# New estimates, a hold-back margin and four column groups in the planner of a hybrid attention and mLSTM kernel

## The chip, the cores and the metric

The kernel runs on one core of a Trainium2 chip. The metric is the device time of one execution in microseconds (us); what counts is the median of several runs.

## The reference, cut to what matters

Two layers work on 2048 latent tokens (`x`) and 256 context tokens (`ctx`), each 1024 wide. In each layer the tokens are normalised and modulated, projected, mixed by two groups of heads that read the same input, and projected back.

```python
for l in range(DEPTH):                                    # DEPTH = 2
    mod_x = split(silu(c)     @ w_ada[l] + b_ada[l], 3)   # shift, scale, gate: one row of 3072 each
    mod_c = split(silu(c_ctx) @ w_ada[l] + b_ada[l], 3)
    xn = rmsnorm(x, norm_g) * (1 + scale_x) + shift_x     # the same for ctx
    aq, ak, av, az, mq, mk, mv, mo, mz, mi, mf = project(xn, w_in)
    att = window_ctx_attention(rope(aq), rope(ak), av, ...) * silu(az)   # 8 heads, band of 3 blocks of 128
    cq, ck = silu(conv5(mq, mk))
    m = rmsnorm(sigmoid(mo) * mlstm_both_directions(cq, ck, mv, mi, mf)) * silu(mz)   # 4 heads, chunks of 128
    x = x + gate_x * (concat(att, m) @ w_out)             # ctx likewise, but for the last layer
return rmsnorm(x, final_g)
```

The part named modulation below is the first two lines: two rows (one from `c`, one from `c_ctx`) times a matrix of 1024 x 3072 per layer, in float32.

## The kernel before, in words

Tokens are cut into 18 blocks of 128 (2 of context, 16 latent). Large projections split both operands into two float16 halves and add three products (`mm3`: 8 slices of the contraction times 3, so 24 matmuls).

The order of the work is made by a planner that runs when the program is built (class `Plan`). Each instruction that is issued goes through `op`, which knows a cost for it (`cost`), a clock for each engine (`clk`; E is TensorE, V VectorE (DVE), S ScalarE (ACT), G GpSimd (POOL), Q the DMA queue of SyncE), and the time at which each piece of a tile is written or read. From these it works out when the instruction would start and end; the instruction then takes the next place in its engine's program. So the estimates decide only in what order each engine's instructions stand, never when they start on the chip: there they start when the engine has come to them and their inputs are there.

The work is written as generators. Streams (`stream`) hold TensorE's work: `alpha` (attention, 4 pairs of heads j per layer, each going through 18 or 16 blocks with `qproj`, `score`, `zproj`, `pv`), `beta` (mLSTM, 4 heads per layer, each with `mproj`, that is convolution, v projection and forward state, and then `mmix`, that is the mixing, with `tb_pe`, `zp_pe`, `mix_pe` for each block), `ada` (modulation), `kphase`, `rphase`, `outproj`, and loaders of weights. Tasks (`spawn`) hold what follows a matmul on the other engines. `run_until` lets all tasks go on as far as they can, then takes one step of one stream: of equal priority, the one whose planned TensorE time divided by its weight is least (alpha 308, beta 560, ada 43 in layer 1 and 14 in layer 0's gate part).

A generator that needs a result calls `till`. Before, it lets the generator go on once the planned TensorE clock is within 0.2 us of the planned time of the result. If no stream and no task can go on, the planned TensorE clock jumps to the next time that somebody waits for.

Buffers are counted: PSUM tiles "b" (4) and "d" (2), 8 slots "g" of 4 KB for each partition (weight stages, convolution, modulation's weights, blocks of x), 8 "toz", 15 "p", and so on. `get` takes one, `put` gives it back.

Modulation comes in chunks. Layer 0's scale and shift come first of all, in 8 chunks of 256 columns (tiles `wada`, three buffers of 1 MB); its gate and all of layer 1 are 32 chunks of 128 columns (tiles `g`), run beside the rest. Each chunk multiplies 8 slices of `sc` (128 x 2) by the weight slice in float32 and adds them up in rows 0 and 1 of one PSUM tile; one VectorE instruction adds the bias (`row`), one more multiplies by `norm_g` for the scale, and the row goes to DRAM (`modD`), from where `load_mod` spreads it over the partitions.

All instructions are issued on line 228, in `op`; so they are told apart by their tiles.

Of the kernel before, what the change touches and what calls it, by code (L numbers as in the profile page):

```python
# [13 lines left out]
P = 128  # L14
# [22 lines left out]
def _where(g):  # L37
    out = []
    while g is not None and getattr(g, "gi_frame", None) is not None:
        out.append((g.gi_code.co_name, g.gi_frame.f_lineno))  # L40
        g = g.gi_yieldfrom
    return out

# [77 lines left out]
LAT, WAR = 0.12, 0.12  # L121


class Plan:
# [29 lines left out]
    def cost(self, e, name, a, kw):  # L154
        n = _free(a[0])
        if e == "E":
            if name == "transpose":
                return 0.003 + (n / 1200.0 if a[1].dtype == F32 else 0.03), 0.1
            if kw["rhs"].dtype == F32:
                return max(4 * n, 512) / 2400.0 + 0.005, 0.1  # L160
            return max(n, 64) / 2400.0 + 0.0027, 0.1
# [7 lines left out]
        if e == "S":  # L169
            base = 0.05 if a[1].space == bass.MemoryType.PSUM else 0.11  # L170
            return base + n / 1200.0 + 0.08 * cols + (0.11 if "accum_out" in kw else 0.0), LAT
        if e == "G":
            if name == "memset" or name == "tensor_copy":
                return 0.12 + n / 1600.0, LAT
            if name == "tensor_scalar":
                return 0.18 + n / 1080.0, LAT
            return (0.55 if a[-1] == ALU.pow else 0.14) + n * 2.1e-3, LAT
        if name == "reciprocal":
            n *= 8
        if name == "tensor_tensor_reduce":  # L180
            return 0.25 + n / 960.0, LAT
# [4 lines left out]
    def op(self, e, name, fn, a, kw):  # L186
# [7 lines left out]
        t = self.clk[e]  # L194
# [53 lines left out]

    def take(self, tag, n, shape=None, dtype=None):
# [49 lines left out]
    def stream(self, gen, prio, weight=1.0):  # L299
        self.streams.append([gen, prio, weight, 0.0])  # L300

    def run_until(self, flag):
        idle = 0
        while flag not in self.done:
# [15 lines left out]
            for s in sorted(self.streams, key=lambda s: (s[1], s[3] / s[2])):  # L320
# [7 lines left out]
                s[3] += self.now - t0  # L328
# [28 lines left out]
class Kern(Plan):  # L357
# [240 lines left out]
    def ada(self, l, parts, width, tags):  # L598
# [46 lines left out]
        for i, (j, n) in enumerate(todo):  # L645
# [5 lines left out]
            for k in range(KT):  # L651
                self.mm(ps[:2, :width], self.sc[:, k, :], wt[:, k, :], start=(k == 0), stop=(k == KT - 1))
# [383 lines left out]
    def attention(self, l, j):  # L1036
# [194 lines left out]
        yield from qproj(pairs[0])  # L1231
        prev = None
        for n, b in enumerate(blocks):
            yield from score(b, 0)
            yield from zproj(b)
# [4 lines left out]
            if n % 2 == 0 and n + 2 < len(blocks):  # L1240
                yield from qproj(pairs[n // 2 + 1])
            if b == blocks[-8 if len(blocks) > 8 else 0]:
                self.done.add(("wa soon", l, j))
            if b == blocks[-1]:
                self.put(wt)
# [13 lines left out]
    def mproj(self, l, h):  # L1259
# [127 lines left out]
        box["stored", 0] = True  # L1387
        for b in range(NT + 1):
            if b < NT:
                gi, o = self.grp(b)  # L1390
                ps = yield from self.get("b")
                yield from self.mm3(ps[:, :P], lambda a, k: XT[gi][:, a, k, o:o + P], lambda a, k: wv[:, a, k, :], 8)
                self.spawn(keep(b, ps))
                yield True
            if b == NT - 1:
                self.put(wv)
# [37 lines left out]
    def mmix(self, l, h):  # L1434
# [207 lines left out]

        yield from tb_pe(0)
# [9 lines left out]
        self.put(wt)  # L1653
# [307 lines left out]
    def run(self):  # L1961
# [4 lines left out]
        with ExitStack() as es:  # L1966
            self.open(es)
            with tc.manual_schedule():
# [8 lines left out]
                self.at = es.enter_context(tc.tile_pool(name="at", bufs=1))  # L1977
                self.stream(self.alpha(), 2, W_ALPHA)
# [56 lines left out]
```

## Time and profile before

| what | value |
|---|---|
| median of 3 runs | 2718.24 us (2717.17 to 2721.46) |
| the profiled execution's own time | 2717.66 us |
| its span, first to last instruction | 2715.9 us |
| around the span | 1.76 us |
| mean granted TensorE clock | 0.963 of full speed |

Busy time is the time in which at least one instruction of an engine runs. "Idle before" an instruction is what the engine waited just ahead of it, and the name behind the arrow is what ended the wait. PE is TensorE's matmuls, PEld its weight loads.

### The profile page before, as it was taken

The page shows a single profiled execution, that of the slowest core. Times are in us where ns is not written, and L with a number is a line of the kernel's source. Part 1 is how long each engine was busy: PE and PEld are TensorE (multiplying, and loading weights), DVE is VectorE, ACT ScalarE, POOL GpSimd, SP SyncE. Part 2 cuts the span into 40 slices and gives each one's busy share as a digit, 9 for nine tenths or more (in the row PEclk, how much of TensorE's full clock was granted, in tenths as well). Part 3 has the DMA queues.
Part 4 walks back from the last instruction along what each step waited for, and adds up shares of the span by engine and source line. Part 5 has one row for each costly group of instructions (what it writes and reads, how often), then busy time and mean ns, then how long its engine had stood idle before and what let it go on. Part 6 is the DMA issues. An engine that isn't in the chain of part 4 may idle for free.

```text
span 2715.9 us, 64740 instructions
## 1 busy us (share of the span) xinstructions
PE 2433.4 (90%) x23650; PEld 1882.5 (69%) x23650; DVE 1856.7 (68%) x4817; ACT 1498.1 (55%) x3788; POOL 1522.0 (56%) x2832
## 2 busy tenths in 40 slices
PE   6699999999999999886897889999899998998898
PEld 2577887788778877883453458876886887787543
DVE  4979666856675657587774667758666865867674
ACT  1446675757665756673222246766675765667321
POOL 1937478547764865475122463787288468727411
PEclk9799999999999999998898989999999999999999
DMA  8365774576658744678994536744764674467684
GB/s 260 102 168 117 146 137 91 123 156 126 111 109 160 138 105 89 120 167 247 215 199 113 144 87 121 150 102 90 142 130 85 130 150 94 82 142 160 189 219 122
DMA packets 822448, 376.16 MB, mean 139 GB/s; under 512 B 492537, under 2 KB 800241, under 8 KB 821105
## 3 DMA queue, kind: packets, MB, share of 16 engines
q1 hardware_dynamic: 822128, 372.02, 61.7%
q8 instruction: 186, 3.05, 0.5%
q14 instruction: 134, 1.09, 0.1%
HBM read 198.99 MB, written 57.56 MB: 94 GB/s over the span
## 4 chain that ended last, share of the span: by engine, by line
PE 37%; DVE 13%; POOL 8%; DMA 8%; ACT 5%; issue 5%; SPq 1%; POOLq 0%; ACTq 0%; DVEq 0%
PE b L228 35%; DVE g L228 3%; POOL g L228 2%; POOL mb L228 2%; POOL p L228 2%; DVE d L228 2%; PE d L228 1%; DVE ph L228 1%; DVE toz L228 1%; DVE held L228 1%; POOL held L228 1%; DMA pp<-ph 1%; DMA g<-in_w_out 1%; DMA cs<-in_rope 1%; ACT g L228 1%
## 5 line engine op out<-in xcount | busy, mean ns | idle before, releaser
L228 PEld LDWEIGHTS <-xt 128*128 128x128 f16 x11856 | 880.0, 99 | 223.3 <-issue 46.3
L228 PE MATMUL b<-woz,xt 128*128 128x256 f16 (+2 forms) x3824 | 484.4, 276 | 21.1 <-DVE p L228 13.2
L228 PE MATMUL b<-xt,wqk 128*128 128x512 f16 (+1 forms) x1824 | 388.7, 365 | 0.1
L228 POOL TENSOR_TENSOR held<-held,mhalf 128x1 f32<-128x1 f32 x200 | 120.0, 600 | 332.5 <-DVE held L228 329.8
L228 PEld LDWEIGHTS <-wqk 128*128 128x128 f16 x1824 | 175.7, 99 | 160.3 <-issue 3.3
L228 ACT ACTIVATE d<-d,smx,un 128x640 f32<-128x640 f32 (+2 forms) x272 | 223.9, 823 | 101.4 <-DVE smx L228 82.8
L228 POOL TENSOR_TENSOR p<-p 128x128 f32<-128x128 f32 x272 | 131.3, 483 | 257.8 <-ACT p L228 221.0
L228 DVE SCALAR_TENSOR_TENSOR ph<-d,ph 128x640 f16<-128x640 f32 (+2 forms) x272 | 212.0, 780 | 79.7 <-ACT ph L228 78.0
L228 PE MATMUL b<-wa,xt 128*128 128x128 f16 (+1 forms) x3328 | 250.7, 224 | 11.3 <-DVE toz L228 4.7
L228 PE MATMUL b<-wv,xt 128*128 128x128 f16 x3456 | 228.2, 219 | 9.6 <-DVE s L228 7.1
L228 POOL TENSOR_TENSOR g<-g,mb 128x512 f32<-128x512 f32 (+1 forms) x152 | 192.4, 1266 | 34.1 <-ACT g L228 20.2
L228 DVE CUSTOM_DVE_ANT_0 d<-d,mask 128x640 f32<-128x640 f32 (+1 forms) x240 | 195.9, 816 | 20.5 <-PE d L228 19.9
L228 PE MATMUL b<-xt,wa 128*128 128x256 f16 x1632 | 203.0, 274 | 2.5 <-DVE s L228 1.6
L228 POOL TENSOR_TENSOR toz<-toz,cs 128x256 f32<-128x256 f32 x160 | 124.3, 797 | 135.5 <-DMA cs<-in_rope 100.2
L228 PE MATMUL d<-ks,toz 128*128 128x256 f16 (+1 forms) x1568 | 186.8, 255 | 11.9 <-DVE toz L228 7.8
L228 ACT ACTIVATE ph<-d 128x640 f16<-128x640 f32 (+2 forms) x272 | 182.7, 672 | 13.1 <-DMA pp<-ph 6.2
L228 PEld LDWEIGHTS <-wa 128*128 128x128 f16 x1696 | 162.8, 99 | 31.2 <-ACT wa L228 5.8
L228 DVE TENSOR_TENSOR toz<-toz 64x256 f16<-64x256 f32 (+2 forms) x234 | 134.4, 575 | 64.1 <-POOL toz L228 37.1
L228 PEld LDWEIGHTS <-toz 128*128 128x128 f16 x1568 | 145.0, 98 | 39.2 <-DVE toz L228 11.9
L228 DVE SCALAR_TENSOR_TENSOR g<-g,cw 128x512 f32<-128x512 f32 (+1 forms) x152 | 143.4, 944 | 35.4 <-POOL g L228 32.5
L228 DVE SCALAR_TENSOR_TENSOR s<-s,gc,b 128x129 f32<-128x129 f32 x272 | 94.1, 346 | 105.4 <-ACT p L228 68.3
L228 DVE TENSOR_REDUCE held<-g 128x1 f32<-128x1024 f32 x110 | 132.8, 1210 | 26.4 <-DMA g<-in_w_out 13.4
(243 smaller groups left out, 5297.5 us busy)
## 6 DMA issues: line engine op xcount, KB each, us to landing
mb<-mD SPq DMA_DIRECT2D x136, 256.0 KB
g<-in_w_in SPq DMA_DIRECT2D x60, 512.0 KB
cs<-in_rope SPq DMA_DIRECT2D x80, 256.0 KB
mixD<-p SPq DMA_DIRECT2D x272, 64.0 KB
g<-mixD SPq DMA_DIRECT2D x34, 512.0 KB
g<-in_w_ada SPq DMA_DIRECT2D x32, 512.0 KB
g<-in_x SPq DMA_DIRECT2D x24, 512.0 KB
cfD<-s SPq DMA_DIRECT2D x136, 64.5 KB
```

What stands on the lines that cost most here:

```text
L228: fn(*a, **kw)
```

## The change

- `cost`, ScalarE and VectorE and POOL: base costs are raised (ScalarE from PSUM 0.05 to 0.065, from SBUF 0.11 to 0.12, 64 rows 0.1 more; POOL's `tensor_scalar` 0.18 to 0.27; VectorE's 64-row `tensor_tensor` 0.18 instead of 0.065 for its fixed part; and two smaller ones). A matmul's result is seen 0.215 us after its end instead of 0.1.
- `cost`, TensorE: a float32 matmul whose stationary operand has two columns (modulation) is charged a quarter.
- `op`: an instruction whose inputs come late starts 0.03 us (POOL) or 0.02 us (TensorE) after them.
- `till`: a generator goes on when the planned TensorE clock is 0.3 us past the planned time of the result, instead of 0.2 us before it.
- `ada`: the eight slices of a chunk go to four column groups of the array (PSUM rows 0, 32, 64 and 96, two slices each), and three further VectorE instructions add up the four partial rows.
- `Piece` wraps `qproj`, `zproj`, the v projection and `zp_pe`. The lists `qa` and `qb` are filled, and nothing reads them; `may`, `spare` and the `owner` of a stream are called by nothing or change nothing. The pieces run at their old places. Weight tiles are given back when their last piece is through: for `zp_pe` one `mix_pe` earlier, for attention a `score`, a `pv` and (but for the last block) nothing else earlier.

```diff
+MARGIN = 0.3
...
             if name == "transpose":
-                return 0.003 + (n / 1200.0 if a[1].dtype == F32 else 0.03), 0.1
+                return 0.003 + (n / 1200.0 if a[1].dtype == F32 else 0.03), 0.215
             if kw["rhs"].dtype == F32:
-                return max(4 * n, 512) / 2400.0 + 0.005, 0.1
-            return max(n, 64) / 2400.0 + 0.0027, 0.1
+                t = max(4 * n, 512) / 2400.0 + 0.005
+                return t / 4 if _free(kw["lhsT"]) == 2 else t, 0.215
+            return max(n, 64) / 2400.0 + 0.0027, 0.215
...
-            base = 0.05 if a[1].space == bass.MemoryType.PSUM else 0.11
+            base = 0.065 if a[1].space == bass.MemoryType.PSUM else 0.12
+            if a[0].shape[0] == 64:
+                base += 0.1
...
             if name == "tensor_scalar":
-                return 0.18 + n / 1080.0, LAT
+                return 0.27 + n / 1080.0, LAT
...
         if name == "tensor_tensor_reduce":
-            return 0.25 + n / 960.0, LAT
+            return 0.3 + n / 1040.0, LAT
+        if name == "tensor_tensor" and a[0].shape[0] == 64:
+            return 0.18 + n / 960.0, LAT
+        if name == "tensor_scalar" and n == 1 and cols > 1:
+            return 0.19, LAT
...
-        t = self.clk[e]
+        t = 0.0
...
+        t = max(self.clk[e], t + (0.03 if e == "G" else 0.02 if e == "E" else 0.0))
...
-    def till(self, *aps, slack=0.2):
+    def till(self, *aps):
         t = max(self._times(self.wr, v) for v in aps)
-        while t > self.now + slack:
-            yield t - slack
+        while t > self.now - MARGIN:
+            yield t + MARGIN
...
             V.tensor_tensor(row, ps[:2, :width], bt[:, 0], ALU.add)
+            for g in (32, 64, 96):
+                V.tensor_tensor(row, ps[g:g + 2, :width], row, ALU.add)
             self.put(ps)
...
             for k in range(KT):
-                self.mm(ps[:2, :width], self.sc[:, k, :], wt[:, k, :], start=(k == 0), stop=(k == KT - 1))
+                g = 32 * (k % 4)
+                self.mm(ps[g:g + 2, :width], self.sc[:, k, :], wt[:, k, :], start=(k < 4), stop=(k >= 4))
...
+        qp = [Piece(qproj(b), lambda: self.spare(toz=4, b=1), then) for b in pairs]
+        zp = [Piece(zproj(b), lambda: self.spare(p=5, b=1), then) for b in blocks]
...
-        yield from qproj(pairs[0])
+        yield from qp[0].all()
...
-            yield from zproj(b)
+            yield from zp[n].all()
...
-                yield from zp_pe(i)
+                yield from zp[i].all()
```

## Rows read from the trace of the kernel before

**Rows 1.** The page's first part: busy time, share of the span and number of instructions of each engine.

```profile
PE 2433.4 (90%) x23650; PEld 1882.5 (69%) x23650; DVE 1856.7 (68%) x4817; ACT 1498.1 (55%) x3788; POOL 1522.0 (56%) x2832
```

**Rows 2.** The windows view by stages. Columns: stretch in us, its length, busy time of PE, PEld, DVE, ACT and POOL with instructions in brackets, the granted TensorE clock, the share of the DMA engines, GB/s.

```profile
0.00:50.00 50.00, 33.97 (x149) 13.21 (x149) 21.02 (x63) 6.38 (x9) 4.04 (x16) 1.00 0.79 238
50.00:200.00 150.00, 111.78 (x1033) 91.07 (x1034) 120.01 (x254) 66.33 (x114) 89.56 (x128) 0.85 0.55 161
200.00:1200.00 1000.00, 943.83 (x10302) 791.65 (x10300) 681.29 (x1940) 649.18 (x1744) 644.59 (x1199) 0.99 0.61 125
1200.00:1300.00 100.00, 60.68 (x440) 41.27 (x437) 75.46 (x190) 42.55 (x102) 54.11 (x111) 0.83 0.87 230
1300.00:1550.00 250.00, 222.65 (x1329) 120.61 (x1330) 150.99 (x265) 62.31 (x93) 65.67 (x132) 0.94 0.73 169
1550.00:1650.00 100.00, 75.98 (x675) 53.36 (x673) 75.66 (x165) 44.86 (x90) 71.69 (x71) 0.90 0.38 87
1650.00:2500.00 850.00, 789.35 (x8742) 671.93 (x8740) 597.23 (x1682) 568.84 (x1528) 533.06 (x1009) 0.98 0.60 121
2500.00:2550.00 50.00, 39.01 (x273) 28.91 (x271) 33.05 (x91) 24.47 (x67) 38.33 (x89) 0.90 0.65 165
2550.00:2700.00 150.00, 150.00 (x697) 67.90 (x696) 96.43 (x165) 32.07 (x43) 19.29 (x73) 1.00 0.70 192
```

**Rows 3.** What TensorE waited for between 200 and 1200 us (the three longest of twelve): us in total, times, longest.

```profile
PE b L228 <- DVE p L228: 14.3, 16, 2.3
PE b L228 <- DMA p<-qD: 7.4, 3, 3.7
PE b L228 <- DVE s L228: 5.7, 6, 2.1
```

**Rows 4.** The same between 1600 and 2500 us (the three longest of fourteen).

```profile
PE b L228 <- DVE p L228: 13.3, 12, 2.3
PE b L228 <- DVE s L228: 10.1, 9, 2.8
PE b L228 <- DVE toz L228: 9.4, 7, 2.7
```

**Rows 5.** Modulation's matmuls and weight loads over the whole span, by shape: busy us, mean ns of one, idle before.

```profile
L228 PE MATMUL b<-g,sc 128*2 128x128 f32 x512 | 62.8, 281 | 13.1 <-DMA g<-in_w_ada 11.7 <-ACT V L228 0.7 <-DVE s L228 0.5
...
L228 PEld LDWEIGHTS b<-g,sc 128*2 128x2 f32 x512 | 43.0, 87 | 30.6 <-DMA g<-in_w_ada 9.1 <-issue 4.9 <-ACT V L228 0.9
...
L228 PE MATMUL b<-wada,sc 128*2 128x256 f32 x128 | 30.8, 405 | 0.0
```

**Rows 6.** TensorE's instructions in order of time around one chunk of modulation: start, length of the group, tiles, shape, count.

```profile
257.80 0.67 PE L228 MATMUL b<-wv,xt 128*128 128x128 f16 x9
258.40 1.91 PE L228 MATMUL b<-g,sc 128*2 128x128 f32 x16
260.24 1.02 PE L228 MATMUL b<-vp,pp 128*128 128x128 f16 x20
261.10 0.28 PE L228 MATMUL b<-ident,kT 128*128 128x128 f32 x1
```

**Rows 7.** All engines in order of time in the first stage, the rows of the chunks of 256 columns and of one later chunk.

```profile
27.66 17.43 PE L228 MATMUL b<-wada,sc 128*2 128x256 f32 x80
...
45.63 0.41 DVE L228 TENSOR_TENSOR row<-b,bt 2x256 f32<-2x256 f32 x1 [3.11 <-DMA modD<-row]
...
56.34 7.23 PE L228 MATMUL b<-g,sc 128*2 128x128 f32 x48 [8.92 <-DMA g<-in_w_ada]
```

**Rows 8.** The windows view in steps of 5 us, four of them; columns as in rows 2.

```profile
15.00:20.00 5.00, 5.00 (x16) 1.55 (x14) 0.04 (x1) 0.35 (x2) 0.00 (x0) 1.00 1.08 373
20.00:25.00 5.00, 5.00 (x30) 2.11 (x29) 3.96 (x10) 2.30 (x4) 0.56 (x1) 1.00 0.85 270
...
40.00:45.00 5.00, 5.00 (x24) 1.82 (x22) 1.64 (x4) 0.00 (x0) 0.00 (x0) 1.00 0.61 208
...
115.00:120.00 5.00, 4.34 (x57) 4.01 (x55) 5.00 (x5) 1.85 (x3) 4.59 (x9) 1.00 0.01 2
```

**Rows 9.** VectorE's instruction that adds the bias, by shape: busy us, mean ns, idle before.

```profile
L228 DVE TENSOR_TENSOR row<-b,bt 2x128 f32<-2x128 f32 x32 | 8.8, 275 | 32.4 <-PE b L228 22.5 <-DMA modD<-row 9.9
...
L228 DVE TENSOR_TENSOR row<-b,bt 2x256 f32<-2x256 f32 x8 | 3.3, 412 | 17.8 <-DMA modD<-row 11.0 <-PE b L228 6.8
```

**Rows 10.** Four kinds of instruction whose estimate changes, by shape.

```profile
L228 DVE TENSOR_TENSOR toz<-toz 64x256 f16<-64x256 f32 x136 | 82.7, 608 | 18.4 <-ACT toz L228 14.6
...
L228 ACT ACTIVATE toz<-toz 64x256 f16<-64x256 f32 x136 | 55.9, 411 | 19.2 <-DVE toz L228 17.1
L228 POOL TENSOR_SCALAR toz<-toz 128x128 f32<-128x128 f32 x136 | 44.4, 326 | 19.1 <-ACT toz L228 18.8
L228 POOL TENSOR_SCALAR held<-held 128x1 f32<-128x1 f32 x188 | 36.3, 193 | 16.5
```

**Rows 11.** TensorE in order of time at the end of attention in layer 0 (the last `pv` is the row with `vp,pp`).

```profile
1220.05 0.84 PE L228 MATMUL b<-vp,pp 128*128 128x128 f16 x16
1222.91 0.30 PE L228 MATMUL b<-ident,kT 128*128 128x128 f32 x1 [2.01 <-DVE toz L228]
...
1237.36 0.39 PE L228 MATMUL b<-s,mb 128*128 128x129 f32 x2
```

**Rows 12.** The windows view of the stretch in which layer 1's mLSTM runs without attention; columns as in rows 2.

```profile
2508.00:2536.00 28.00, 21.75 (x174) 18.69 (x173) 21.32 (x58) 16.25 (x45) 22.35 (x44) 0.88 0.49 140
```

More of the change, by code (lines that the diff above doesn't have):

```diff
@@ L42, in _where, with __init__, may, step @@
     return out
+class Piece:
+    def __init__(self, gen, may, then=None):
+        self.gen, self.free, self.then, self.begun, self.over = gen, may, then, False, False
+    def may(self):
+        return self.begun or self.free()
+    def step(self):
+        self.begun = True
+        try:
+            return next(self.gen)
+        except StopIteration:
+            self.over = True
+            if self.then:
+                self.then()
+            return True
+    def all(self):
+        while not self.over:
+            r = self.step()
+            if not self.over:
+                yield r
 class Eng:
@@ L247, in get, with spare @@
         return self.new(tag, shape, dtype)
+    def spare(self, **left):
+        return all(self.spec[t][3] - self.cnt[t] > n for t, n in left.items())
     def take(self, tag, n, shape=None, dtype=None):
@@ L297, in spawn, with stream @@
         self.tasks.append(gen)
-    def stream(self, gen, prio, weight=1.0):
-        self.streams.append([gen, prio, weight, 0.0])
+    def stream(self, gen, prio, weight=1.0, owner=None):
+        s = [gen, prio, weight, 0.0]
+        s.append(owner or s)
+        self.streams.append(s)
+        return s
     def run_until(self, flag):
@@ L327, in run_until @@
                     break
-                s[3] += self.now - t0
+                s[4][3] += self.now - t0
                 if r is True:
@@ L1230, in attention, with then @@
         xt_done()
-        yield from qproj(pairs[0])
+        todo = [len(pairs) + len(blocks)]
+        def then():
+            todo[0] -= 1
+            if todo[0] == 0:
+                self.put(wt)
+        qp = [Piece(qproj(b), lambda: self.spare(toz=4, b=1), then) for b in pairs]
+        zp = [Piece(zproj(b), lambda: self.spare(p=5, b=1), then) for b in blocks]
+        for n in range(len(blocks)):
+            if n % 2 == 0:
+                self.qa.append(qp[n // 2])
+            self.qa.append(zp[n])
+        yield from qp[0].all()
         prev = None
@@ L1240, in attention @@
             if n % 2 == 0 and n + 2 < len(blocks):
-                yield from qproj(pairs[n // 2 + 1])
+                yield from qp[n // 2 + 1].all()
             if b == blocks[-8 if len(blocks) > 8 else 0]:
                 self.done.add(("wa soon", l, j))
-            if b == blocks[-1]:
-                self.put(wt)
             prev = b
@@ L1387, in mproj, with vproj @@
         box["stored", 0] = True
+        def vproj(b):
+            gi, o = self.grp(b)
+            ps = yield from self.get("b")
+            yield from self.mm3(ps[:, :P], lambda a, k: XT[gi][:, a, k, o:o + P], lambda a, k: wv[:, a, k, :], 8)
+            self.spawn(keep(b, ps))
+            yield True
+        vp = [Piece(vproj(b), lambda: self.spare(b=1), (lambda: self.put(wv)) if b == NT - 1 else None)
+              for b in range(NT)]
+        self.qb += vp
         for b in range(NT + 1):
             if b < NT:
[L1390 to L1396, printed above, removed]
+                yield from vp[b].all()
             c = b - 2
@@ L1641, in mix_pe, with then @@
                 yield True
+        todo = [sum(full)]
+        def then():
+            todo[0] -= 1
+            if todo[0] == 0:
+                self.put(wt)
+        zp = [Piece(zp_pe(i), lambda: self.spare(toz=3, p=5, b=1), then) if full[i] else None for i in range(NT)]
+        self.qb += [z for z in zp if z]
         yield from tb_pe(0)
```

4 lines of the change are left out of this document (2 added, 2 removed).

## The prediction, made before the changed kernel ran

> **What bounds the kernel now.** I read the page's busy times first, then the windows by stages, then TensorE's waits in the two long stages, and last the instructions that the change touches. TensorE is busy for 2433.4 us, 90% of the span, and VectorE comes next with 68% [rows 1]. The reader is to see in the windows that this 90% is a mean over unlike stages [rows 2]. Where attention and mLSTM run side by side, TensorE is busy 943.83 us of 1000 in layer 0 and 789.35 of 850 in layer 1. The end is wholly TensorE's, 150.00 of 150. The lost time lies in the start (50 - 33.97 = 16 us, then 150 - 111.78 = 38 us), in the turn from layer 0 to its output projection (100 - 60.68 = 39 us), in the start of layer 1 (24 us) and its end (11 us). So TensorE sets the pace of the two long stages: what shortens its work there, or its 56.2 + 60.7 = 117 us of idle time, shortens the kernel, and an instruction more on VectorE (681.29 of 1000 us) costs nothing there. Between 50 and 200 us it is the other way round: VectorE is full, 5.00 us of 5 at 115 us [rows 8].
>
> The waits of the long stages are many and short: the largest kinds are 14.3 us in 16 waits and 13.3 us in 12 [rows 3, 4], about 1 us each, and none of those listed is over 3.7 us. TensorE came to an instruction whose input was late by about a microsecond.
>
> **The column groups, TensorE's side.** A chunk of 128 columns holds 16 matmuls with 16 weight loads: 512 of each for 32 chunks [rows 5]. There are 8 slices in a chunk, so each float32 product is a pair of matmuls, each with its own weights. One chunk takes from 258.40 to 260.24, that is 1.84 us or 0.115 us for each matmul [rows 6]. The change puts neighbouring slices, not the two matmuls of a pair, into different column groups. If the engine starts matmuls in the order in which they stand, the second of a pair waits until the first has left its group, and only the step to the next slice is quick. No row shows two column groups at work, so I bound the quick step. From above: 0.115 us, nothing gained. From below, the quickest stream nearby: the 20 `vp,pp` matmuls from 260.24 to 261.10, 0.043 us each [rows 6]. I take the lower end for the step between slices (it is the nearest row that shows how fast loads and matmuls follow each other) and the upper one within a pair: 8 x 0.115 + 8 x 0.043 = 1.26 us, 0.58 us less for each chunk. Three chunks run at 56 us beside a wait for their own load [rows 7]; 29 lie behind 150 us, most in the stage that TensorE bounds: 29 x 0.58 = 17 us gained. Were all four groups to work at once, a chunk would take 16 x 0.043 = 0.69 us, and the gain would be 29 x 1.15 = 33 us.
>
> The planner charges a quarter, which is more than I expect to be saved. The Trainium skill, "TensorE: Matmul & The Clock Gate" (section on packing small matmuls), says that matmuls keep the order of the program at their start and end, and gives 2.38 times for three column tiles. By the first of these a pair holds the next slice back; by the second, carried over to four groups as an estimate, a chunk would take about 1.84 / 3 = 0.6 us. The sum would come to 2673 us by the first and to about 2656 by the second; no row here shows which holds when each product is a pair.
>
> **The column groups at the start.** Layer 0's chunks of 256 columns run without a break from 27.66 to 45.09, 80 matmuls at 0.218 us [rows 7]. With the same reasoning a chunk of 16 goes from 3.49 to 8 x 0.218 + 8 x 0.043 = 2.09 us, 1.4 us less, for six chunks 8 us. The loads allow less than that. They moved 373 GB/s between 15 and 20 us, when the buffers were still free, and then 270 down to 208 [rows 8]. The mean of these two over the 25 us to 45 is 239 GB/s or 6.0 MB, which at 373 takes 16 us: 9 us less at the very best, with no gap between loads. TensorE will wait for loads part of the time, and I take half of its own 8 us, 4 us, with bounds of 0 and 8.
>
> **The column groups, VectorE's side.** Each chunk gains three instructions like the one that adds the bias: 0.275 us for 128 columns and 0.412 for 256 [rows 9]. In all 32 x 3 x 0.275 + 8 x 3 x 0.412 = 36 us more on VectorE. In the long stages TensorE's work covers it. It shows in two places. The last chunk of the start stands on the path to `modD` [rows 7]: 3 x 0.412 = 1.2 us lost. And between 50 and 200 us, where VectorE is full [rows 8], three chunks with 3 x 0.275 each cost up to 2.5 us. The PSUM tile is held 0.8 us longer, one of four "b"; if TensorE ran out of them, up to 0.8 us a chunk, 26 us, would go, but in the long stages the waits listed are for results, so I put nothing. SP's queue has the `modD` transfers with the next load behind them; they come 0.8 us later a chunk, which the chunks already loaded cover.
>
> **The margin and the hops.** `till` now lets a generator go on 0.5 us later in planned time. TensorE's instructions that wait for another engine stand about 0.5 us of other TensorE work further back; so do their followers on ScalarE, VectorE, POOL and SP, where all shift alike and order changes little. Nothing is added on the chip: no wait and no instruction. What is late by less than 0.5 us is then covered by work of the other stream. With 117 us of idle time in pieces of about 1 us there are some 115 waits; at most 0.5 us of each, 57 us, can go. Longer waits keep their rest, and a chain that stands further back is later itself at its next step. I take half, 28 us. The bounds are 57 us gained and, if the later chains take it all back, 0; a loss is the rival below.
>
> The new estimates help in the same direction, and I count them in these 28 us. VectorE's 64 x 256 instruction takes 0.608 us; the planner said 0.332 and will say 0.447. ScalarE's takes 0.411: 0.323 becomes 0.433. POOL's `tensor_scalar` takes 0.326 for 128 columns and 0.193 for one: 0.299 and 0.181 become 0.389 and 0.271 [rows 10], so the latter two overshoot. The order is nearer to the chip's on some engines, further off on one.
>
> **The rest.** The pieces run at their old places, and nothing reads the lists; the earlier return of weight tiles is worth one `mix_pe` of lead on a load, and no row of the long waits names a weight load: nothing. The turns between the stages are re-shuffled by any change of order; I put them at nothing, with 15 us either way in the range.
>
> **The sum.** 17 + 4 - 1.2 - 2.5 + 28 = 45 us gained. The profiled execution took 2717.66 us, its span 2715.9 and 1.76 around it; the median is 2718.24, 0.6 above. 2717.66 - 45 = 2673 us.
>
> **The rivals.**
> *All four groups work at once.* Then 33 + 8 in place of 17 + 4, so 2673 - 20 = 2653 us. For it: the groups touch different rows of the result and different weights. Against it: the pairs [rows 5].
> *The groups bring nothing* (0 for both TensorE terms): 2673 + 21 = 2694 us. Rows 6 show what may eat the gain: no stream of loads and matmuls there runs faster than 0.043 us a step, and a pair of weights must still be loaded for each product.
> *The margin brings nothing*, since the lateness moves along with the chains: 2673 + 28 = 2701 us. For it: the waits are for chains of several engines, and 2 us waits are among them [rows 3, 4].
> *Slower: mLSTM is left alone at the end of the layers.* Each block of the mixing passes through TensorE twice in a chain that carries a state; standing 0.5 us further back at each, mLSTM falls behind attention. It already ends last: attention's last product in layer 0 starts at 1220.05, mLSTM's at 1237.36 [rows 11], and in layer 1 it runs alone for 28 us, with TensorE busy 21.75 of them [rows 12]. Alone there is nothing to fill its waits: 22% of the time is lost. A head takes about 250 us, since four fill the 1000 us of layer 0 [rows 2]; if 100 us, less than half of one, are left over in each layer, that is 2 x 100 x 0.22 = 44 us, and the margin's 28 us are gone too: 2673 + 28 + 44 = 2745 us. With the margin's gain gone, 17 us are left (2718 - 2701), and it decides the sign once mLSTM runs alone for 17 / 0.22 = 77 us more than now. Against it: the planner shares by TensorE time used, waiting isn't charged, and so mLSTM gets its turn as soon as it can use it.
>
> **How the numbers follow.** Forecast 0.45, four groups at once 0.14, groups without gain 0.12, margin without gain 0.15, slower 0.14. The forecast's own range is 2650 to 2697 (the margin's 0 to 57 us around 28). To leave out no more than 2 in 10 I go from 2625, where four groups, the margin's upper bound and a lucky turn come together in part, to 2735, most of the way to the slower case. This kernel's measurement can't tell changes under 0.2%, 5.4 us. Faster by more than that are the first three cases and nearly all of the fourth with some lost to the turns: 0.78. Within it 0.08, slower 0.14.
>
> **What would show it.** Right: a chunk of 16 modulation matmuls in about 1.3 us instead of 1.84 (0.7 for four at once, 1.8 for none); the start's last `wada` matmul some 4 us earlier; four row instructions a chunk on VectorE; TensorE's idle time in the two long stages down from 117 to about 90 us, with the same producers named and shorter waits; its busy time there down by the 17 us. The prediction is wrong if the idle time doesn't fall, if mLSTM runs alone for far more than 17 and 28 us at the ends of the layers, or if a turn between stages moves by more than 15 us.

## The result, and the profile after

The changed kernel takes 2684.84 us, the median of 4 runs (2681.65 to 2690.49), beside 2717.7 (2716.54 to 2721.46) for the kernel before: 0.9879 of its time, interval 0.986 to 0.9898. It is 33 us or 1.2% faster. The forecast was 2673, with 2625 to 2735 as its range. The profiled execution has a span of 2679.9 us against 2715.9, 36 us less, at the same granted clock (0.963 over the span in both).

First the page's busy line, which answers to [rows 1].

```profile
PE 2394.1 (89%) x23650; PEld 1855.9 (69%) x23650; DVE 1900.0 (71%) x4937; ACT 1500.7 (56%) x3788; POOL 1516.5 (57%) x2832
```

TensorE works 39 us less, VectorE 43 us more, in 120 more instructions. The span shrank by about what TensorE's work did, which invites a simple story. The windows by stages, which answer to [rows 2] and have its columns, speak against it.

```profile
0.00:50.00 50.00, 19.00 (x149) 5.81 (x149) 31.43 (x88) 6.39 (x9) 3.87 (x16) 1.00 0.80 238
50.00:200.00 150.00, 112.60 (x1056) 89.11 (x1057) 124.26 (x266) 68.79 (x117) 93.74 (x133) 0.90 0.53 156
200.00:1200.00 1000.00, 921.96 (x10278) 774.63 (x10275) 721.63 (x2037) 649.56 (x1748) 641.30 (x1200) 0.98 0.60 127
1200.00:1300.00 100.00, 76.54 (x539) 51.65 (x540) 63.77 (x168) 40.32 (x98) 50.96 (x105) 0.85 0.81 209
1300.00:1550.00 250.00, 229.03 (x1422) 127.05 (x1420) 176.09 (x323) 76.03 (x114) 99.53 (x156) 0.96 0.74 185
...
1650.00:2500.00 850.00, 776.07 (x8428) 660.07 (x8427) 595.27 (x1688) 566.69 (x1522) 555.26 (x1081) 0.98 0.60 122
```

In the long stage of layer 0 TensorE is busy 922 us of 1000 where it was 943.83, for 10278 matmuls where it had done 10302: the work became shorter, and the stretch did not hold more of it. In the next two rows it gets through more: 539 matmuls against 440, and 1422 against 1329. That is where the time was gained.

Three instructions that both kernels run once date it. The first matmul of layer 0's output projection (`xt,g`) starts at 1243.61 us, 8 us earlier than the 1251.80 of before. The first matmul on layer 1's gates (`ident,gt`) comes at 1546.43 against 1586.64: the stretch between the two fell from 334.8 to 302.8 us, by 32. All that follows, to the end of the span, takes 1133.5 us against 1129.3. Both kernels have run 13434 matmuls when the gates start, so the same work lies on either side. So the 36 us are 8 up to the first matmul of the output projection, 32 from there through the turn and the projection, and 4 are given back in the rest. Here is the turn, TensorE in order of time, first before, then after.

```profile
1251.80 1.46 PE L228 MATMUL b<-xt,g 128*128 128x512 f16 x3 [6.27 <-DMA g<-g]
...
1302.85 4.30 PE L228 MATMUL b<-xt,wv 128*128 128x256 f16 x24 [23.07 <-DMA xt<-xt]
...
1586.64 0.39 PE L228 MATMUL b<-ident,gt 128*72 128x128 f32 x2 [1.29 <-DVE gt L228]
```

```profile
1243.61 1.67 PE L263 MATMUL b<-xt,g 128*128 128x512 f16 x7
...
1267.52 0.39 PE L263 MATMUL b<-s,mb 128*128 128x129 f32 x2
...
1287.86 0.59 PE L263 MATMUL b<-woz,g 128*128 128x512 f16 x1 [9.59 <-DMA woz<-xt]
...
1292.75 4.05 PE L263 MATMUL b<-xt,wv 128*128 128x256 f16 x24 [0.60 <-DMA xt<-g]
...
1546.43 0.38 PE L263 MATMUL b<-ident,gt 128*72 128x128 f32 x2 [1.26 <-DVE gt L263]
```

Before, TensorE stood for 23 us ahead of the first key projection of layer 1 (`xt,wv`), whose transposed input had not landed, though the output projection was far from done. After, that wait is 0.60 us, and one of 9.59 stands ahead of a step of the output projection. mLSTM's end in layer 0 (`s,mb`) is 30 us later than before (1237.36 in [rows 11]), and the output projection's first blocks now run beside it.

### The profile page after: what moved, and what is told of

Same layout as the page of the kernel before. It is cut to its first block, busy times and chain, and to the rows that moved or that the text cites. A ratio compares the mean times of both kernels' runs of the same rounds, so it can differ in the third digit from the quotient of the medians.

```text
span 2679.9 us, 64870 instructions
## 1 busy us (share of the span) xinstructions
PE 2394.1 (89%) x23650; PEld 1855.9 (69%) x23650; DVE 1900.0 (71%) x4937; ACT 1500.7 (56%) x3788; POOL 1516.5 (57%) x2832
## 5 line engine op out<-in xcount | busy, mean ns | idle before, releaser
L263 PE MATMUL b<-woz,xt 128*128 128x256 f16 (+2 forms) x3808 | 477.4, 276 | 32.7 <-DVE p L263 18.5
L263 DVE TENSOR_TENSOR toz<-toz 64x256 f16<-64x256 f32 (+2 forms) x234 | 140.4, 600 | 41.8 <-POOL toz L263 26.7
L263 PE MATMUL b<-xt,xt 128*128 128x512 f16 x672 | 148.3, 384 | 12.5 <-DMA xt<-xt 12.5
```

What stands on the lines that cost most here:

```text
L263: fn(*a, **kw)
```

## The experiments

Twelve kernels ran, each against the kernel before on the same chip. Three questions: which part brings the time, does TensorE's shorter modulation reach the end, and what is the turn worth?

**Parts of the change, alone and left out.** The groups alone (with the three additions, all seen by the planner; modulation is charged in full, as before):

```diff
+            for g in (32, 64, 96):
+                V.tensor_tensor(row, ps[g:g + 2, :width], row, ALU.add)
...
-                self.mm(ps[:2, :width], self.sc[:, k, :], wt[:, k, :], start=(k == 0), stop=(k == KT - 1))
+                g = 32 * (k % 4)
+                self.mm(ps[g:g + 2, :width], self.sc[:, k, :], wt[:, k, :], start=(k < 4), stop=(k >= 4))
```

> The kernel before with the four column groups alone; estimates and hold-back as before, modulation charged in full. In the changed kernel a chunk of 128 columns takes 0.55 us (311.15 to 311.70) instead of 1.84, so 29 chunks give 37 us of TensorE's time. Theory 1, the groups carry the whole gain: 2718 - 33, so 2680 to 2690 us. Theory 2, as the prediction sized it (groups a third to a half, margin the rest): 2695 to 2703. Theory 3, the saved time turns into idle time unless the estimates change with it: 2710 to 2718.

Measured: 2738.95 us, 1.0067 [1.005, 1.0085]. Slower by 19 us; none of the three theories had a loss.

The hold-back alone:

```diff
+MARGIN = 0.3
...
-    def till(self, *aps, slack=0.2):
+    def till(self, *aps):
         t = max(self._times(self.wr, v) for v in aps)
-        while t > self.now + slack:
-            yield t - slack
+        while t > self.now - MARGIN:
+            yield t + MARGIN
```

> The kernel before with the hold-back of 0.3 us alone (till past the planned time instead of 0.2 us ahead of it). Theory 1: no gain, 2712 to 2724 us, and TensorE's idle time between 200 and 1200 us stays near 56 us. Theory 2: 2685 to 2695 us and some 14 us less idle time there.

Measured: 2743.27 us, 1.0082 [1.0067, 1.0098]. Slower by 23 us, where the prediction had it bring 28; neither theory had a loss of that size.

The changed kernel without the groups (the product into rows 0 and 1, no additions, full charge):

```diff
-                return t / 4 if _free(kw["lhsT"]) == 2 else t, 0.215
+                return t, 0.215
...
-            for g in (32, 64, 96):
-                V.tensor_tensor(row, ps[g:g + 2, :width], row, ALU.add)
...
-                g = 32 * (k % 4)
-                self.mm(ps[g:g + 2, :width], self.sc[:, k, :], wt[:, k, :], start=(k < 4), stop=(k >= 4))
+                self.mm(ps[:2, :width], self.sc[:, k, :], wt[:, k, :], start=(k == 0), stop=(k == KT - 1))
```

> The changed kernel without the column groups and with modulation charged in full: what remains is the estimates, the hops and the hold-back. Theory 1: 2712 to 2724 us, as before. Theory 2: 2690 to 2700 us. Theory 3, the parts only work together: over 2700 us, and g_only too.

Measured: 2703.4 us, 0.9932 [0.9912, 0.9952].

The changed kernel with the old `till`:

```diff
-    def till(self, *aps):
+    def till(self, *aps, slack=0.2):
         t = max(self._times(self.wr, v) for v in aps)
-        while t > self.now - MARGIN:
-            yield t + MARGIN
+        while t > self.now + slack:
+            yield t - slack
```

> The changed kernel with the old till (0.2 us ahead). Theory 1: 2680 to 2690 us, the same as the changed kernel. Theory 2, the hold-back is worth its 28 us: 2705 to 2715 us. A time under 2680 would say that the hold-back costs.

Measured: 2691.21 us, 0.9884 [0.9865, 0.9903], not to be told from the changed kernel's 0.9879. Neither part has the same worth in both settings: the groups cost 19 us alone and, together with the quarter charge, bring 14 in the changed kernel (0.9932 to 0.9879 of 2720); the hold-back costs 23 alone and next to nothing there. No run has the quarter charge alone. It moves modulation: in the kernels that have it the last chunk comes at 567 to 583 us, in all others at 1070 to 1116. This is what TensorE waited for most between 200 and 1200 us (us in all, times, longest): in the hold-back alone, in the changed kernel without it, in the changed kernel, and in the changed kernel without the groups; [rows 3] has 14.3 in 16.

```profile
PE b L229 <- DVE p L229: 27.8, 18, 4.0
```

```profile
PE b L263 <- DVE p L263: 15.7, 15, 2.5
```

```profile
PE b L263 <- DVE p L263: 30.3, 22, 5.6
```

```profile
PE b L263 <- DVE p L263: 15.0, 20, 2.0
```

The first and the third, with the hold-back, wait twice as long for `p`. But the fourth has it too and waits no longer than before, so these waits can't be put down to the hold-back.

**The estimates, and a re-ordering with no meaning.** All new estimates, hops and the late start, without hold-back, pieces and groups (cut to some of its lines):

```diff
-                return 0.003 + (n / 1200.0 if a[1].dtype == F32 else 0.03), 0.1
+                return 0.003 + (n / 1200.0 if a[1].dtype == F32 else 0.03), 0.215
...
-                return 0.18 + n / 1080.0, LAT
+                return 0.27 + n / 1080.0, LAT
...
-        t = self.clk[e]
+        t = 0.0
...
+        t = max(self.clk[e], t + (0.03 if e == "G" else 0.02 if e == "E" else 0.0))
```

> The kernel before with the new estimates alone: the hop of 0.215 us, the raised costs on ScalarE, VectorE and POOL and the later start after late inputs; no column groups, old hold-back, modulation charged in full. Hold-back alone gave 2743 us, groups alone 2739, both against 2720; estimates with hold-back 2703. Theory A, the estimates carry the gain: 2690 to 2705 us, most of it between the end of mLSTM in layer 0 and the start of layer 1 (349 us before, 319 with estimates and hold-back). Theory B, no part has a value of its own and each re-ordering draws a new time: anywhere from 2690 to 2740. Theory C, estimates and hold-back need each other: 2715 to 2740.

Measured: 2678.8 us, 0.9823 [0.9792, 0.9854]. With no instruction changed, it is faster than the changed kernel, and faster than any of its three theories had it.

TensorE's hop alone, 0.1 to 0.215 in each of its three lines (one shown):

```diff
-            return max(n, 64) / 2400.0 + 0.0027, 0.1
+            return max(n, 64) / 2400.0 + 0.0027, 0.215
```

> The kernel before with the later sight of TensorE's results alone (0.215 us instead of 0.1). Theory A with the hop as its core: the same as est_only within 8 us. Theory A with the other costs as its core: 2712 to 2725. Theory B: unrelated to est_only.

Measured: 2739.22 us, 1.0058 [1.0041, 1.0076].

Then one constant that is tied to no duration, the weight by which the planner shares TensorE between the streams, changed by a third of a per cent, in the kernel before and in the changed one:

```diff
-W_ALPHA = 308.0
+W_ALPHA = 307.0
```

> A re-ordering without a meaning: the kernel before with attention's weight 307 instead of 308. If the time of a plan is set by what its rules are worth, 2715 to 2725 us. If a plan's time scatters with every re-ordering (theory B), it can lie 15 to 25 us off.

Measured: 2703.36 us, 0.9908 [0.9877, 0.9939].

> The same for the changed kernel: weight 307 instead of 308. Without scatter 2680 to 2690 us; with scatter of the size that theory B needs, up to 2710.

Measured: 2708.45 us, 0.9936 [0.9909, 0.9962]. The same step takes 20 to 25 us off the kernel before (by the medians and by the ratio) and adds 16 to 24 to the changed one (0.9879, 2684.84). So a new order alone can move this kernel by about 20 us in either direction, and the four runs of parts above cannot be read as the worth of a part. A part's own worth needs an order that stays.

**The groups in an order that stays.** The kernel before, with the planner told of the old product and of no additions, so that the instructions of TensorE, ScalarE, POOL and SP stand in exactly the order of before:

```diff
+            for g in (32, 64, 96):
+                self.nc.vector.tensor_tensor(row, ps[g:g + 2, :width], row, ALU.add)
...
-                self.mm(ps[:2, :width], self.sc[:, k, :], wt[:, k, :], start=(k == 0), stop=(k == KT - 1))
+                def four(out, lhsT, rhs, start, stop, k=k, ps=ps):
+                    g = 32 * (k % 4)
+                    self.nc.tensor.matmul(ps[g:g + 2, :width], lhsT=lhsT, rhs=rhs, start=(k < 4), stop=(k >= 4))
+                self.op("E", "matmul", four, (ps[:2, :width],),
+                        dict(lhsT=self.sc[:, k, :], rhs=wt[:, k, :], start=(k == 0), stop=(k == KT - 1)))
```

> The kernel before in its own order, instruction for instruction on TensorE, ScalarE, POOL and SP: the four column groups and the three added VectorE instructions of each chunk are hidden from the planner, so no plan changes. If TensorE's work bounds the long stages, the 37 us saved there and a few in the start come out: 2678 to 2688 us. If something else sets the pace of a stage, the saved time becomes idle time: 2705 to 2720. If the added VectorE work shows, over 2722.

Measured: 2729.24 us, 1.0018 [1.0008, 1.0029]. TensorE's window of the long stage in this run, beside 943.83 before:

```profile
200.00:1200.00 1000.00, 917.36 (x10234) 771.41 (x10233) 701.89 (x2010) 644.41 (x1731) 640.29 (x1191) 0.98 0.60 124
```

26 us less of work stand in the window, and the time is a fifth of a per cent longer: the third case of the forecast. I followed the two traces matmul by matmul along the identical order between 200 and 1240 us. The 26 chunks there run through 34 us sooner (1.3 us each). Against that, TensorE's waits grow by 27 us, 11 of them directly behind a chunk. Another 12 us go because the other matmuls run more slowly: 1.2 GHz was granted for 48 us of that stretch instead of 24 (the window shows a granted clock of 0.98, where before has 0.99). TensorE ends 4 us behind. One of the waits, all engines in order of time:

```profile
258.23 0.62 PE L656 MATMUL b<-g,sc 128*2 128x128 f32 x16
258.78 1.02 PE L228 MATMUL b<-vp,pp 128*128 128x128 f16 x20
...
261.90 0.27 DVE L228 TENSOR_TENSOR row<-b,bt 2x128 f32<-2x128 f32 x1
262.20 0.93 DVE L632 TENSOR_TENSOR row<-b,row 2x128 f32<-2x128 f32 x3
...
263.18 0.33 PE L228 MATMUL b<-ident,kT 128*128 128x128 f32 x1 [1.41 <-DVE row L632]
```

The chunk is done 1.5 us sooner than in [rows 6], but VectorE reads its result at its old place in the order, then takes 0.93 us for the three additions, and the next user of that PSUM tile waits 1.41 us for the last of them. In the kernel before, this matmul started at 262.78 without a wait: TensorE was 1.46 us ahead after the chunk and is 0.40 us behind here. Such waits for `row` are few by name (4 in that stage, 4.2 us); larger are those for two other chains of VectorE:

```profile
PE d L228 <- DVE toz L228: 10.6, 6, 5.2
PE b L228 <- DVE held L228: 10.5, 8, 2.9
...
PE b L228 <- DVE row L632: 4.2, 4, 1.4
```

Before, these two chains took 4.5 us in 5 waits and 3.6 in 4. The traces tell where this comes from. At 23 of the 26 chunks VectorE loses 0.8 to 1.1 us on the kernel before between the instruction ahead of the additions and the one behind them: it had no idle time there to take them up. Of the longer waits, 22 us end with a result of VectorE that came later than in the kernel before, and 5 with the additions themselves. Some of that lateness is the slower clock's. Here is the longest wait and what follows it, before and with the groups hidden:

```profile
860.55 0.72 PE L228 MATMUL d<-ks,toz 128*128 128x256 f16 x6 [1.12 <-DVE toz L228]
861.11 1.50 PE L228 MATMUL b<-wa,xt 128*128 128x128 f16 x24
```

```profile
867.27 1.25 PE L228 MATMUL d<-ks,toz 128*128 128x256 f16 x6 [5.24 <-DVE toz L228]
868.31 2.77 PE L228 MATMUL b<-wa,xt 128*128 128x128 f16 x24
```

While TensorE waits, the granted clock falls to 0.5 (from 864.4 to 871.3 us), and the same 24 matmuls take 2.77 us instead of 1.50. So the work was exchanged: TensorE's became shorter, and VectorE's additions and the clock took it back. What the shorter modulation would be worth without the additions no run shows.

The same on the order of the new estimates:

> The new estimates alone (2679 us in the earlier run) with the column groups hidden in the same way, so in that kernel's own order. If the groups are worth their TensorE time in any order: 2640 to 2650 us. If they are worth nothing: 2675 to 2685. This is also the candidate for the fastest kernel of the study.

Measured: 2675.08 us, 0.9819 [0.9801, 0.9837]; the estimates alone had 0.9823. TensorE's busy time in the long stage, estimates alone and with the groups under the same order:

```profile
200.00:1200.00 1000.00, 947.45 (x10323) 795.38 (x10321) 687.11 (x1954) 649.33 (x1751) 631.75 (x1196) 0.99 0.59 126
```

```profile
200.00:1200.00 1000.00, 928.42 (x10363) 780.15 (x10355) 716.37 (x2042) 653.37 (x1762) 637.62 (x1207) 0.98 0.61 127
```

19 us less work, and no difference in time that the intervals part. Between 200 and 1240 us the chunks give 33 us here, the waits take 19 and the clock 9 (1.2 GHz for 51 us instead of 28). In two fixed orders the groups cost 5 us and bring nothing that can be told. est_g_hidden has the lowest time of the study; its interval ends below the changed kernel's, but it can't be told from the estimates alone.

**The turn.** The kernel before with one thing moved: layer 1's first key projection is not planned until the fourth block of layer 0's output projection is through. TensorE's order is that of before up to the place of that projection (1302.85 us there).

```diff
...
+            if l and gi == 0:
+                yield from self.need(("on", l - 1, 3))
```

> The kernel before, with layer 1's first projection of keys held back until the fourth block of layer 0's output projection is through. Up to that place the order is the one of before. In the trace of before TensorE waits 23.07 us there for a transposing transfer, while the output projection has work left. If the plan put that projection too early, the wait goes and the time falls by 15 to 23 us, to 2697 to 2706 us. If the output projection waits for the same chain anyway, 2715 to 2725 us.

Measured: 2685.61 us, 0.9857 [0.9835, 0.9878]. Two added lines bring 38 us, as much as the whole change, and 11 us more than the forecast's best case. The windows of the turn and of the output projection behind it, before, in this run, and in the changed kernel:

```profile
1240.00:1320.00 80.00, 45.58 (x248) 23.45 (x249) 54.15 (x108) 21.03 (x30) 23.45 (x37) 0.77 0.80 214
1320.00:1545.00 225.00, 200.53 (x1190) 107.73 (x1189) 139.60 (x245) 56.27 (x82) 64.08 (x128) 0.95 0.73 169
```

```profile
1240.00:1320.00 80.00, 62.26 (x295) 29.79 (x296) 58.52 (x111) 19.93 (x24) 24.93 (x40) 0.87 0.90 245
1320.00:1545.00 225.00, 211.27 (x1351) 119.62 (x1350) 161.38 (x287) 67.05 (x103) 86.78 (x150) 0.97 0.74 175
```

```profile
1240.00:1320.00 80.00, 67.53 (x381) 36.16 (x379) 49.56 (x109) 23.06 (x40) 37.37 (x70) 0.91 0.80 226
1320.00:1545.00 225.00, 207.50 (x1322) 117.22 (x1320) 158.14 (x289) 66.17 (x98) 88.39 (x145) 0.95 0.73 177
```

TensorE gains 17 us of work in the first row and 11 in the second, nearly what the changed kernel gains (22 and 7). The place of the projection shows in the waits: before, 23.07 us ahead of `xt,wv` at 1302.85; here

```profile
1298.52 0.59 PE L228 MATMUL b<-woz,xt 128*128 128x512 f16 x1 [4.41 <-DVE g L228]
...
1312.59 4.07 PE L228 MATMUL b<-xt,wv 128*128 128x256 f16 x24 [2.90 <-DVE g L228]
```

Layer 1's gates come at 1545.16, as in the changed kernel (1546.43). Of the 38 us the trace puts 20 on this wait (23.07 to 2.90); the others come with the new order behind that place, and a share of them can be scatter.

Where layer 1's gates start (`ident,gt`) puts the profiled executions nearly in the order of their times. The second column is the first matmul of layer 0's output projection. The execution of the changed kernel with the old `till` is the slowest of its five, so its ratio doesn't go with its row.

| run | output projection, us | gates of layer 1, us | time of the same execution, us | ratio of the medians |
|---|---|---|---|---|
| one move at the turn | 1248.5 | 1545.2 | 2681.0 | 0.9857 |
| changed kernel | 1243.6 | 1546.4 | 2681.7 | 0.9879 |
| estimates, groups hidden | 1238.9 | 1547.3 | 2675.1 | 0.9819 |
| estimates alone | 1245.4 | 1552.9 | 2682.1 | 0.9823 |
| changed, neighbours in one group | 1254.5 | 1555.8 | 2691.1 | none, one run |
| changed, no groups | 1257.3 | 1561.6 | 2696.1 | 0.9932 |
| changed, old `till` | 1255.5 | 1567.1 | 2702.0 | 0.9884 |
| changed, weight 307 | 1252.0 | 1570.6 | 2708.9 | 0.9936 |
| before, weight 307 | 1257.3 | 1572.5 | 2703.3 | 0.9908 |
| before | 1251.8 | 1586.6 | 2717.7 | 1 |
| groups alone | 1256.0 | 1591.6 | 2735.4 | 1.0067 |
| groups hidden | 1255.4 | 1592.2 | 2726.9 | 1.0018 |
| hops alone | 1275.5 | 1598.6 | 2739.0 | 1.0058 |
| hold-back alone | 1279.8 | 1602.5 | 2745.4 | 1.0082 |

Between the first and the last gates lie 57 us; from the gates to the end all of them take 1126 to 1142 us. Not all of the spread is the turn's: the hops alone and the hold-back alone reach the output projection 24 and 28 us later than the kernel before and make up 12 of them behind it.

**What the four groups do.** The changed kernel with neighbouring slices in the same group, so that four matmuls in a row share one; in strict order 12 of 16 would be held:

```diff
-                g = 32 * (k % 4)
-                self.mm(ps[g:g + 2, :width], self.sc[:, k, :], wt[:, k, :], start=(k < 4), stop=(k >= 4))
+                g = 32 * (k // 2)
+                self.mm(ps[g:g + 2, :width], self.sc[:, k, :], wt[:, k, :], start=(k % 2 == 0), stop=(k % 2 == 1))
```

> The changed kernel with slices 0 and 1 in column group 0, 2 and 3 in group 1 and so on, so that neighbours share a group. It is for the time of one chunk of 16 matmuls: 0.55 us in the changed kernel. If a matmul that waits for its own group lets the next group go ahead, a chunk takes 0.5 to 0.7 us again. If each waits for its turn in the order of the program, half of the steps are slow ones and more: 1.4 to 1.6 us. The time of the whole says little: 2675 to 2715 us.

Measured: 2691.09 us in one run. Its chunk, from the start of its first matmul to the start of what follows, takes 313.39 - 312.82 = 0.57 us:

```profile
312.82 0.64 PE L263 MATMUL b<-g,sc 128*2 128x128 f32 x16
313.39 1.02 PE L263 MATMUL b<-vp,pp 128*128 128x128 f16 x20
```

In the changed kernel it is 0.55:

```profile
311.15 0.62 PE L263 MATMUL b<-g,sc 128*2 128x128 f32 x16
311.70 1.02 PE L263 MATMUL b<-vp,pp 128*128 128x128 f16 x20
```

With 12 of 16 held and 4 quick, at the prediction's prices, the chunk would take 12 x 0.115 + 4 x 0.043 = 1.55 us. Putting neighbours into one group costs 0.02. The starts within the chunk say how. Here is the same chunk of the run with neighbours in one group up to 312.9 and to 313.0 us:

```profile
312.82 0.31 PE L263 MATMUL b<-g,sc 128*2 128x128 f32 x4
```

```profile
312.82 0.42 PE L263 MATMUL b<-g,sc 128*2 128x128 f32 x8
```

The single starts in the trace lie in rounds of four. Within a round the starts lie 0.013 us apart (0.007 in the changed kernel); a round comes 0.109 us behind the one before it in both kernels, which is also the step from matmul to matmul in the single group of before. The trace doesn't name a matmul's group. But one matmul of each group in every round fits both kernels, and four neighbours of one group, each 0.109 us behind the last, do not.

## Why the prediction was right and wrong

The sign, the size and the range held: 2684.84 against 2673, -33 us against -45. The working did not; most of the 45 us was put where nothing was gained, and the place where it was gained was put at nothing.

**"The second of a pair waits until the first has left its group" (1.26 us a chunk): wrong.** A chunk takes 0.55 us where it took 1.84: the rival of all four groups at once, and below its 0.69, since a step to another group takes 0.007 us and not the 0.043 that I had as the lower end. The Trainium skill's rule of strict order ("TensorE: Matmul & The Clock Gate", section on packing small matmuls), by which I chose against that rival, is not what these two chunks show; the Trainium skill's figure carried over, 0.6 us, was the nearer.

**"TensorE sets the pace of the two long stages", and "an instruction more on VectorE … costs nothing there" (17 us, 33 by the rival): together wrong, and the main fault.** The work did go: the chunks in the long stage of layer 0 run through 34 us sooner in the fixed order. The time didn't fall (1.0018, and 0.9819 beside 0.9823). Waits took 27 us back, most of them for results of VectorE, which lost about a microsecond at nearly every chunk's additions, and the lower clock took 12. A busy share of 94% was read as the bound, and one of 68% as room at any place. Whether TensorE's time would come out if VectorE had nothing added stays open. The page had a view that I didn't weigh, the shares of the chain that ended last in the kernel before:

```profile
PE 37%; DVE 13%; POOL 8%; DMA 8%; ACT 5%; issue 5%; SPq 1%; POOLq 0%; ACTq 0%; DVEq 0%
```

Other engines and transfers have 34% beside TensorE's 37% (13 + 8 + 8 + 5). The chain is followed back only to 651 us, and it holds the end of the kernel, where TensorE is alone; from 651 to 1200 us TensorE has 32% of it, VectorE 19, transfers 16, POOL 13 and ACT 12.

**The additions, and the tile held 0.8 us longer, "I put nothing": sized well, and wrong that they cost nothing.** The additions came as forecast: 36 us forecast, and the rows of after, which answer to [rows 9] (us in all, mean ns), give 27.5 + 10.1 = 37.6.

```profile
L263 DVE TENSOR_TENSOR row<-b,row 2x128 f32<-2x128 f32 x96 | 27.5, 286 | 3.3
...
L263 DVE TENSOR_TENSOR row<-b,row 2x256 f32<-2x256 f32 x24 | 10.1, 420 | 0.8
```

But the held tile did stop TensorE, for 1.41 us in the place shown, about what the chunk had saved there. By name it is only 4.2 us of the stage, far from the 26 that I had as its upper bound; most of the rest of the waiting ended with later results of VectorE, as said above.

**The start, 4 us: the step held, the gain went at once.** TensorE's last `wada` matmul comes at 40.6 us instead of 44.7, and it now waits for the loads, as forecast. Its rows of the first stage in the changed kernel:

```profile
36.42 1.89 PE L263 MATMUL b<-wada,sc 128*2 128x256 f32 x16 [4.05 <-DMA wada<-in_w_ada]
39.35 1.88 PE L263 MATMUL b<-wada,sc 128*2 128x256 f32 x16 [1.04 <-DMA wada<-in_w_ada]
46.90 0.48 PE L263 MATMUL b<-ident,held 128*128 128x128 f32 x1 [5.67 <-DVE held L263]
...
56.12 1.03 PE L263 MATMUL b<-g,sc 128*2 128x128 f32 x16 [8.74 <-DMA g<-in_w_ada]
```

TensorE's busy time in the first 50 us fell from 33.97 to 19.00 us. Yet the transpose of `held` starts at 46.90 (47.10 before), and the next chunk at 56.12 (56.34 in [rows 7]), after its own load: of 4 us on TensorE, 0.2 are left behind the VectorE chain and the load that come next.

**The margin, half of what it could cover, 28 us: wrong.** TensorE's idle time in layer 0's long stage was to fall, and rose from 56 to 78 us, by just as much as its work fell. Without the groups, hold-back and estimates together leave it at 55 us (no_groups, busy 944.81 of 1000); the hold-back alone raises it to 68 (busy 931.86). The rival "the margin brings nothing" was right as to its sum (no_margin, 0.9884 beside 0.9879); alone it cost 23 us. The new estimates, counted within these 28 us, brought 44 us alone (0.9823 of 2723), more than the change. By the traces most of that is at the turn: the gates of layer 1 come 34 us earlier, 6 of them up to the first matmul of the output projection, and the long stage's idle time goes from 56 to 53 us only. The hop among them, alone, costs 16 us. So little is seen of truer estimates covering lateness; they made an order in which the turn came out well, and why it did so is not shown.

**"The turns between the stages … nothing, with 15 us either way": wrong, and here lie 32 of the 36 us.** The windows [rows 2] showed 39 idle us in the turn's 100, and I named them and passed on. The 23 us wait behind them was there to be found, and its price too: one move in the plan brings 38 us, 20 of them on this wait.

**mLSTM left alone: it came in layer 0, not by the hold-back, and the price didn't come.** It ends 37 us after attention there instead of 17 (last `s,mb` at 1267.52, last `vp,pp` at 1230.24). With the hold-back alone it is 13 us, with the estimates alone, which have none, 45. And the output projection fills it from 1243.61 on. In layer 1 it runs alone for 24 us instead of 28.

Three figures don't follow from the prediction's own terms. With the margin at 0 or 57 us around 28 the forecast's own range is 2644 to 2701, not 2650 to 2697; the Trainium skill's figure, in the same sum, gives 2654, not 2656; and "VectorE is full" holds for the window at 115 us, while over 50 to 200 us it is busy for 120.01 of 150. None of them moves the forecast.

The written test was met on its own terms: idle time that doesn't fall and a turn that moves by more than 15 us were named as what would show the reasons wrong, and both came. The time was right by luck, through a re-ordering whose size I had not known: a weight moved from 308 to 307 moves it by 16 to 25 us.

## What to carry to other kernels

A high busy share alone doesn't show a bound, and a lower one on another engine doesn't show room: here 34 us of TensorE's work were exchanged for additions on VectorE, and nothing came out. Before crediting a faster instruction on the busiest engine, ask what its successor waits for, and test it in an order that stays (issue the new work while the planner still counts the old). Look at the granted clock too, which can take back a part. Where a planner writes the order, measure first what a meaningless nudge of one constant does; here that is about 20 us, and no part under that size can be judged by switching it on or off. Look for the gain in the longest single wait beside work that could run, above all where one stage hands over to the next: one move for the sake of a 23 us wait brought as much as the whole change.

## What the chip showed that was not expected

**Column groups pass one another.** 16 small float32 matmuls in four groups took 0.55 us instead of 1.84, and 0.57 us with neighbours in the same group: the starts come in rounds of four, 0.109 us apart, so a matmul that is held up by its own group seems to let those of other groups pass, at least in this shape.

**The granted clock fell where TensorE had less to do, in some kernels.** The stretch from 30 to 40 us, in the kernel before, in the changed kernel and with the groups hidden (columns as in rows 2):

```profile
30.00:40.00 10.00, 10.00 (x48) 3.95 (x47) 2.56 (x7) 0.00 (x0) 0.53 (x3) 1.00 0.88 286
```

```profile
30.00:40.00 10.00, 4.43 (x40) 1.15 (x44) 5.98 (x15) 0.00 (x0) 0.00 (x0) 1.00 0.68 217
```

```profile
30.00:40.00 10.00, 4.37 (x44) 1.16 (x44) 6.01 (x15) 0.00 (x0) 0.00 (x0) 0.50 0.68 215
```

The last two do almost the same work, one at 2.4 GHz and one at 1.2. It cost next to nothing: the transpose of `held` starts at 46.90 us in the one and at 47.09 in the other, since TensorE waits for loads and for VectorE there. In the long stage, where TensorE has work to do, the lower clock cost the kernel with the groups hidden 12 us.

**The turn is a stretch of transfers.** In the 36 us up to the early key projection of the kernel before, the DMA engines' share is 0.97, while TensorE is busy for 12.93 us:

```profile
1267.00:1303.00 36.00, 12.93 (x61) 5.84 (x60) 25.46 (x44) 9.93 (x11) 13.54 (x18) 0.71 0.97 257
```
